# First stage of a hybrid attention block: two gates ahead of the memory, and keys written after the gates

## The chip, the cores and the metric

The kernel runs on one core of a Trainium2 chip. The time is that of one execution on the device, in microseconds (us). The core has a matrix engine (TensorE, PE in the profile; its weight loads are PEld), a vector engine (DVE), a scalar engine (ACT), GpSimd (POOL) and SyncE (SP), whose main work here is to issue DMAs. Each engine works through its own instructions in a fixed order and waits on semaphores that others raise. POOL issues some of the DMAs too, on a software queue.

## The reference

One layer for 1024 tokens of 1024 channels. After an RMS norm, one wide projection feeds three mixers and the merge gates; then comes an output projection with a residual, and a gated feed-forward part, which the change does not touch. All values are float32.

```python
h = _rmsnorm(x, norm_mix_g[l])
z = h @ w_in[l]
(hq, hf, hi, hg, fq, fk, fv, ff, mq, gate_logits) = jnp.split(z, pts, axis=-1)
...
mem_kv = _rmsnorm(mem, norm_mem_g[l]) @ mem_kv_w[l]      # 256 memory tokens, keys and values of 512
y_c = _memory_mixer(mq, mem_kv, mem_q_norm_g[l], mem_k_norm_g[l])
gates = jax.nn.sigmoid(gate_logits).reshape(B, T, 3, D_MODEL)
merged = gates[:, :, 0] * (y_a @ w_br_hgrn) + gates[:, :, 1] * (y_b @ w_br_fox) + gates[:, :, 2] * (y_c @ w_br_mem)
```

The 24 chunks of 128 gate channels (three branches of eight) and the queries of the memory mixer are plain projections of the normed x. The norm is applied late: a projection uses x times its gain, and the result is multiplied by the row rx of one scale for each token.

## The kernel before, in words

**Three matmuls for one.** To keep float32 accuracy, each operand is split into a high half (a cast, `cast`, L161, on ACT) and a low half (the difference, `split`, L169, on DVE). One product is then three matmuls in `mm3` (L155 to L157): high by high, high by low, low by high. A matmul here is 128x128 by 128x512. Where x is an operand, its halves are uh and ul (`x_chunk`, L316 on ACT and L317 on DVE), one pair of tiles for each of eight chunks of 128 channels.

**First stage.** The list SEQ sets the order of the steps in the program. In SEQ, k0 to k7 are the eight steps of the memory's projection (`kv_chunk`; four for the keys, four for the values, each with a weight tile wkv of 512 KB), x0 to x7 load and split a chunk of x, g0 and g1 split the weights of the first two gate chunks, s0 to s7 multiply one chunk of x with both (`gate_step`: 12 matmuls into four PSUM banks), mn, mk, mv and xn are the norm of the memory, its keys, its values and the norm of x (the squares of eight row tiles xr, L395, on ACT). All loads stand in one row on SP's queue. The split memory is umh and uml (L305, L306). `mem_keys` scales the keys (L365, L366, L367, L370), transposes them on TensorE (L375), scales them into mkf (L377), and POOL writes them to DRAM as kvd (L378). The values go the same way (L357, L358).

**What follows.** `spread_dma` (L323 to L327) makes the row rx: a transpose of the eight token columns, a copy on ACT, a write to DRAM and a load that repeats it over all partitions. `gate` multiplies a finished PSUM bank with rx (L420, DVE), takes a tanh (L421, ACT), and SP writes the tile gt, one of three, to DRAM (L431, L573). Two more gate chunks (the cover, `gates_early`) are computed while `differences` builds four families of differences of quarters of x, T1 to T4, from the raw tiles xk. Their halves are then operands of `dense_unit`, which computes two chunks of 128 channels at a time with seven products of quarters instead of eight (sums of weights s1 to s4, L474; PSUM snapshots fe, L466; products B11, B21, T1, T2, B22, T3, T4). The weights of a unit are loaded on POOL's queue (L499).

**What sets the order.** The program is recorded in the order of SEQ and of the code, and a scheduler then orders each engine's instructions by its own estimate; `tc.issue_after` keeps an instruction from being placed ahead of another. Tiles with the same tag share buffers, and a pool that is released makes its place free for the next one. The pool p0 of the first stage and the pool ps1 of the dense units lie on the same side: T1 to T4, s1, s2, fe and gt of ps1 come to lie where p0 had row tiles, split memory, mkf and others. Such a reuse is one more wait. In both kernels the place of s1 overlaps that of mkf.

## Time and profile before

| | |
|---|---|
| median of 3 runs | 1707.13 us (1705.72 to 1708.78) |
| profiled execution | 1707.23 us, its span 1705.5 us |
| granted TensorE clock | 1.0 |
| TensorE busy | 99% of the span, 8941 matmuls |
| DVE, ACT, POOL busy | 67%, 47%, 19% |
| DMA | 227.17 MB, mean 133 GB/s |

The span goes from the first to the last instruction. A row of the timeline is: start, duration, engine, line, operation, output and inputs, shapes, and in brackets the idle time just before it with what ended it. The durations of matmuls overlap, since they are pipelined: their pitch is the distance of two starts. On ACT and DVE the distance between starts is about 0.1 us less than a duration. A row by groups has a count, the busy time and the mean in ns. For DMAs, the time to landing is from the issue to the arrival of the last byte.

### The profile page before, as it was taken

Reading aid. Unit: us, or ns where it says so; the run is one execution under the profiler, and the core shown is the slowest. Engines: PE = TensorE matmul, PEld = TensorE weight load, DVE = VectorE, ACT = ScalarE, POOL = GpSimd, SP = SyncE. Lnnn points to the kernel's source line nnn. Section 1 sums busy time; section 2 is a strip of 40 time slices with the busy share of each in tenths; the row PEclk is TensorE's granted clock in tenths of the full one; section 3 lists DMA queues with packets and bytes.
Section 4 is the critical chain, followed back from the end, with each engine's and each line's share of the span. In section 5 each row is a group of like instructions: output and inputs, shape, how many; then the busy total and the mean of one; then the engine's idle time right before and its main releaser. Section 6 shows DMA issues by size and latency. Waiting matters only on the chain.

```text
span 1705.5 us, 24256 instructions
## 1 busy us (share of the span) xinstructions
PE 1689.9 (99%) x8941; PEld 1449.0 (85%) x8941; DVE 1142.3 (67%) x2044; ACT 808.9 (47%) x1436; POOL 325.7 (19%) x419
## 2 busy tenths in 40 slices
PE   8999999999999999999999999999999999999998
PEld 6888899989898998888888888788888888888887
DVE  7656545665666655786856845987787887775654
ACT  8634456655464553776531333644443444533432
POOL 0100022443433331553310000211111111100000
PEclk9999999999999999999999999999999999999999
DMA  9533232221212111100336552566445345494772
GB/s 361 182 132 112 76 133 85 77 92 45 95 53 87 52 57 56 67 28 17 102 128 210 166 185 99 161 174 173 144 146 142 118 141 155 167 357 150 244 273 87
DMA packets 83207, 227.17 MB, mean 133 GB/s; under 512 B 9728, under 2 KB 12424, under 8 KB 83088
## 3 DMA queue, kind: packets, MB, share of 16 engines
q1 hardware_dynamic: 65040, 161.12, 26.8%
q0 software_dynamic: 18048, 64.50, 13.1%
q8 instruction: 70, 1.15, 0.3%
q14 instruction: 49, 0.40, 0.1%
HBM read 180.72 MB, written 67.93 MB: 146 GB/s over the span
## 4 chain that ended last, share of the span: by engine, by line
PE 96%; DMA 2%; DVE 1%; ACT 1%; SPq 0%; issue 0%; POOL 0%; POOLq 0%; ACTq 0%
PE pp L155 21%; PE pp L157 21%; PE pp L156 21%; PE lg L157 4%; PE lg L155 4%; PE lg L156 4%; PE tr L156 2%; PE tr L157 2%; PE tr L155 2%; PE po L877 1%; PE lg L836 1%; PE lg L835 1%; PE po L876 1%; PE po L157 1%; PE po L155 1%; PE po L156 1%
## 5 line engine op out<-in xcount | busy, mean ns | idle before, releaser
L155 PE MATMUL pp<-uh,wh 128*128 128x512 f32 x412 | 163.2, 396 | 0.3 <-ACT wh L161 0.3
L156 PE MATMUL pp<-ul,wh 128*128 128x512 f32 x412 | 162.9, 395 | 0.0
L157 PE MATMUL pp<-uh,wl 128*128 128x512 f32 x412 | 162.4, 394 | 0.0
L156 PE MATMUL pp<-wl,uh 128*128 128x256 f32 (+1 forms) x512 | 146.2, 286 | 0.0
L157 PE MATMUL pp<-wh,ul 128*128 128x256 f32 (+1 forms) x512 | 145.9, 286 | 0.0
L155 PE MATMUL pp<-wh,uh 128*128 128x256 f32 (+1 forms) x512 | 145.5, 285 | 0.0
L161 ACT CAST wh<-s 128x512 fp32r<-128x512 f32 x113 | 68.4, 620 | 155.7 <-PE pp L156 77.6
L161 ACT CAST wh<-raw 128x1024 fp32r<-128x1024 f32 (+2 forms) x76 | 67.5, 890 | 101.3 <-PE pp L156 85.7
L161 ACT CAST wh<-rw 128x512 fp32r<-128x512 f32 x87 | 53.3, 620 | 97.6 <-PE pp L156 58.1
L155 PEld LDWEIGHTS pp<-wh,uh 128*128 128x128 f32 x512 | 97.3, 190 | 1.3
L156 PEld LDWEIGHTS pp<-wl,uh 128*128 128x128 f32 x512 | 97.4, 190 | 0.9
L157 PEld LDWEIGHTS pp<-wh,ul 128*128 128x128 f32 x512 | 97.4, 190 | 0.9
L1369 POOL DMA_DIRECT2D rw<-in_w_up x44 | 24.1, 555 | 384.9 <-ACT sqs L1304 163.0
L161 ACT CAST dwh<-wr 128x1024 fp32r<-128x1024 f32 (+1 forms) x41 | 40.2, 980 | 116.0 <-PE tr L156 39.2
L169 DVE TENSOR_TENSOR wl<-raw,wh 128x1024 fp32r<-128x1024 f32 (+2 forms) x75 | 78.0, 1041 | 22.0 <-ACT wh L161 21.7
L155 PEld LDWEIGHTS pp<-uh,wh 128*128 128x128 f32 x412 | 77.5, 188 | 15.3 <-ACT wh L161 0.7
L157 PEld LDWEIGHTS pp<-uh,wl 128*128 128x128 f32 x412 | 77.5, 188 | 15.1
L156 PEld LDWEIGHTS pp<-ul,wh 128*128 128x128 f32 x412 | 77.5, 188 | 14.5
L851 ACT ACTIVATE pt<-pt,st 128x128 f32<-128x128 f32 (+3 forms) x64 | 49.7, 777 | 39.8 <-DVE st L848 32.8
L169 DVE TENSOR_TENSOR dwl<-wr,dwh 128x1024 fp32r<-128x1024 f32 (+1 forms) x41 | 46.3, 1129 | 30.3 <-ACT dwh L161 30.2
L853 POOL TENSOR_SCALAR pt<-pt,st 128x128 f32<-128x128 f32 (+3 forms) x64 | 51.0, 797 | 78.0 <-DVE st L852 57.6
L161 ACT CAST ph<-tr 128x512 fp32r<-128x512 f32 (+1 forms) x80 | 41.8, 544 | 39.8 <-PE tr L865 14.5
(501 smaller groups left out, 5121.0 us busy)
## 6 DMA issues: line engine op xcount, KB each, us to landing
rw<-in_w_up POOLq DMA_DIRECT2D x44, 512.0 KB, 4.7
sd<-in_w_dn POOLq DMA_DIRECT2D x30, 512.0 KB, 6.0
br<-yd SPq DMA_DIRECT2D x30, 512.0 KB, 5.5
raw<-in_w_cm SPq DMA_DIRECT2D x26, 512.0 KB, 3.4
gd<-gt SPq DMA_DIRECT2D x48, 256.0 KB, 2.0
gt<-gd SPq DMA_DIRECT2D x48, 256.0 KB, 2.7
yd<-fc SPq DMA_DIRECT2D x44, 256.0 KB, 2.5
wr<-sd SPq DMA_DIRECT2D x20, 512.0 KB, 4.5
```

The lines of the kernel that those rows point to most:

```text
L155: PE.matmul(ps, lh, rh, start=first, stop=False, skip_group_check=more)
L156: PE.matmul(ps, lh, rl, start=False, stop=False, skip_group_check=more)
L157: PE.matmul(ps, ll, rh, start=False, stop=last, skip_group_check=more)
L161: return S.copy(out, in_)
L169: return (sub or V).tensor_sub(l, src, h.bitcast(F32))
L835: PE.matmul(ps[:, :w], qa[i][:, tsl], kh[i][:, s0:s0 + w], start=True, stop=False)
L836: fox_sets[p][3] = PE.matmul(ps[:, :w], qa[i][:, tsl], kl[i][:, s0:s0 + w], start=False, stop=True)
L851: S.activation(pt[:, :ns], pt[:, :ns], AF.Exp, bias=st[:, 2:3], accum_out=st[:, 3:4])
L853: G.tensor_scalar(pt[:, :ns], pt[:, :ns], st[:, 3:4], 0.0, ALU.mult, ALU.add)
L876: PE.matmul(o, vhl[:, sb, :], ph[:, src], start=(sb == 0), stop=False)
L877: PE.matmul(o, vhl[:, sb, :], pl[:, src], start=False, stop=last)
L1369: late["raw"] = G.dma_start(raw[:, 2 * i:2 * i + 2, :], src[:, 2 * i:2 * i + 2, :])
```

## The change

The first stage is put in another order and its loads with it.

- Nine matmuls of constants (`dull`) open TensorE's order.
- The two first gate chunks come before the memory. Their weights come as one new input, w_first, with the rows of both chunks for a channel side by side, in parts (`load_first`, `first_weights`); the first two chunks of x come and are split in halves. `gate_step` runs over the halves of the tokens first.
- The memory follows: all of it loaded with one DMA, split in eight steps (u0 to u7), then the eight steps k0 to k7. Row tiles of x have buffers of their own ("row"), four, as have the memory weights ("wkv").
- Four of the eight squares of the rows of x go to DVE (`tensor_tensor_reduce`).
- `mem_keys` is parted: `keys_out` (norm and scale) after the keys' four steps, and the transposes, the scaling into mkf and the write to DRAM at the end of SEQ, after the gates' evaluation.
- The first chunk of the cover is `first_cover`, in SEQ; the transpose for rx stands within it. `first_gates` follows it, all with gt tiles of p0.
- In `differences`, chunks 0 to 3 of x are no longer scaled by the gain. T1's halves take the gain while they are split, and T2 and T3 are formed with the negative gain column ngx.

The order of the built program: on ACT, the six tanh of the third, first and second gate chunks stand before the scaling of the second half of the keys into mkf. On POOL, the keys' write follows the first two weight loads of the dense units and the values' write. On DVE, the sum s1 follows; it waits for the keys' write, in whose place it lies. Behind s1 stand, in order: T1 low 0, s2, T1 low 1, a gate, T1 low 2, a difference for T2, T1 low 3, T3 low 0, a difference, T3 low 1 and 2, a difference, T3 low 3, a sum for T4, the low half of s1's weight.

```diff
...
+NDULL = 9
...
-SEQ = ("k0 k1 k2 k3 x0 x1 g0 x2 mr g1 k4 s0 s1 x3 s2 k5 x4 mn mk s3 k6 x5 s4 k7 mv x6 s5 x7 xn s6 s7").split()
+SEQ = ("w0 x0 s0 w1 x1 s1 w2 x2 s2 x3 s3 w4 x4 s4 x5 s5 x6 s6 x7 s7 u0 u1 u2 u3 mn u4 u5 u6 u7 k0 k1 k2 k3 me k4 k5 k6 k7 mv xn c0 ev mk").split()
+WFIRST = {0: (0, 1), 1: (1, 2), 2: (2, 4), 4: (4, 8)}
...
+    def row_tile(name, tag="wkv"):
+        return p0.tile([P, 2 * HB], F32, tag=tag, name=name, bufs=4)
+
+    for tag in ("row", "wkv"):
+        for i in range(4):
+            row_tile(f"{tag}{i}", tag)
+    umh = p0.tile([P, KC, NM], F32R, tag="umh", name="umh")
+    uml = p0.tile([P, KC, NM], F32R, tag="uml", name="uml")
+    mkf = p0.tile([P, 4, NM], F32, tag="mkf", name="mkf")
     mt = p0.tile([P, KC, NM], F32, tag="mt", name="mt")
-    def row_tile(name):
-        return p0.tile([P, 2 * HB], F32, tag="wkv", name=name, bufs=6)
-
-    wkv = [row_tile(f"wkv{q}") for q in range(4)]
-    mem_row = [row_tile(f"mr{i}") for i in range(2)]
-    wkv += [row_tile(f"wkv{q}") for q in range(4, 8)]
-    x_row = [row_tile(f"xr{i}") for i in range(6)]
-    x_row += [row_tile(f"xr{i}") for i in (6, 7)]
+
+    G.memset(mhalf, -0.5)
+    dull = p0.tile([P, P], F32, tag="line", name="dull")
+    G.memset(dull, 0.0)
+    for _ in range(NDULL):
+        PE.matmul(ps_tr()[:, :P], mhalf[:, 0:1].to_broadcast([P, P]), dull, start=True, stop=True)
+
+    wg = [row_tile(f"wg{i}") for i in range(2)]
+
+    def load_first(k):
+        k0, k1 = WFIRST[k]
+        sl = slice((k0 % 4) * 256, (k1 - 1) % 4 * 256 + 256)
+        SP.dma_start(wg[k // 4][:, sl], w_first[k // 4][:, sl])
+
+    def load_x(k, parts=1, between=None):
+        for i in range(parts):
+            sl = slice(i * T // parts, (i + 1) * T // parts)
+            SP.dma_start(xk[k][:, sl], xT[:, k, sl])
+            if between and i == 0:
+                between(k)
+
+    def load_wkv(q):
+        wkv.append(row_tile(f"wkv{q}"))
+        late["wkv"] = SP.dma_start(wkv[q], w_mkv[q])
+
+    def load_row(i):
+        nonlocal last_row
+        x_row.append(row_tile(f"xr{i}", "row"))
+        last_row = SP.dma_start(x_row[i], x_rows[i])
...
+    load_x(0, 2, load_first)
+    load_first(1)
+    load_x(1, 2)
+    load_first(2)
+    load_x(2)
+    load_first(4)
+    load_x(3)
+    load_x(4)
+    load_x(5)
+    load_x(6)
+    load_x(7)
+    SP.dma_start(mt, memT)
+    for i in range(2):
+        mem_row.append(row_tile(f"mr{i}"))
+        SP.dma_start(mem_row[i], mem_rows[i])
+    load_wkv(0)
+    load_wkv(1)
     SP.dma_start(ones, mats[:, P:P + 1])
-    rgw = []
-    for what in SEQ:
-        if what[0] == "x" and what != "xn":
-            k = int(what[1])
-            SP.dma_start(xk[k], xT[:, k, :])
-        elif what == "mr":
-            for i in range(2):
-                SP.dma_start(mem_row[i], mem_rows[i])
-        elif what[0] == "g":
-            br, j = order[int(what[1])]
-            rgw.append(raw_weights(w_cm[16 + 8 * br + j], KC * P))
-        elif what in ("k4", "k5", "k6", "k7"):
-            q = int(what[1])
-            SP.dma_start(wkv[q], w_mkv[q])
     SP.dma_start(ident, mats[:, 0:P])
-    for i in range(8):
-        last_row = SP.dma_start(x_row[i], x_rows[i])
-    G.memset(mhalf, -0.5)
+    for i in range(4):
+        load_row(i)
+    load_wkv(2)
+    load_wkv(3)
+    for i in range(4):
+        load_row(4 + i)
+        load_wkv(4 + i)
+    br, j = order[2]
+    cover_raw = raw_weights(w_cm[16 + 8 * br + j], KC * P)
...
+    def mem_chunk(k):
...
-        late["x_cast"] = S.activation(uh[k], xk[k], AF.Copy, scale=col(C_GX + k))
-        V.scalar_tensor_tensor(out=ul[k], in0=xk[k], scalar=col(C_GX + k), in1=uh[k].bitcast(F32),
-                               op0=ALU.mult, op1=ALU.subtract)
-
-    def spread_dma(r, rcol, row, name):
-
-        ps = ps_tr()
+        parts = 2 if k < 2 else 1
+        for i in range(parts):
+            sl = slice(i * T // parts, (i + 1) * T // parts)
+            S.activation(uh[k][:, sl], xk[k][:, sl], AF.Copy, scale=col(C_GX + k))
+            late["x_low"] = V.scalar_tensor_tensor(out=ul[k][:, sl], in0=xk[k][:, sl], scalar=col(C_GX + k), in1=uh[k][:, sl].bitcast(F32),
+                                   op0=ALU.mult, op1=ALU.subtract)
...
+    keys = []
+
+    def keys_out():
...
+        keys.append(mkt)
+
+    def mem_keys():
+        mkt = keys[0]
...
+    gps = [[ps_lg(), ps_lg()], [ps_tr(), ps_po()]]
+    gw = {}
+
+    def first_weights(k):
+        k0, k1 = WFIRST[k]
+        if k % 4 == 0:
+            gw[k // 4] = [wp.tile([P, 4 * 264], F32R, tag=t, name=t, bufs=3) for t in ("wh", "wl")]
+        sl = slice((k0 % 4) * 256, (k1 - 1) % 4 * 256 + 256)
+        split(S, gw[k // 4][0][:, sl], gw[k // 4][1][:, sl], wg[k // 4][:, sl])
 
     def gate_step(k):
-        for i in range(2):
-            for n in range(2):
+        h, l = gw[k // 4]
+        for n in range(2):
+            for i in range(2):
                 sl = slice(n * HB, (n + 1) * HB)
-                mm3(gps[i][n], gw[i][0][:, k, :], gw[i][1][:, k, :], uh[k][:, sl], ul[k][:, sl], k == 0, k == KC - 1)
+                ws = slice((k % 4) * 256 + i * P, (k % 4) * 256 + (i + 1) * P)
+                mm3(gps[i][n], h[:, ws], l[:, ws], uh[k][:, sl], ul[k][:, sl], k == 0, k == KC - 1)
...
+            if i % 2:
+                V.tensor_tensor_reduce(out=x_row[i], in0=x_row[i], in1=x_row[i], op0=ALU.mult, op1=ALU.add, scale=1.0,
+                                       scalar=0.0, accum_out=rt[:, i:i + 1])
+            else:
+                late["square"] = S.activation(x_row[i], x_row[i], AF.Square, accum_out=rt[:, i:i + 1])
...
+    cover = gates_early(NCOVER - 1)
+
+    def first_cover():
+        wh, wl = weights(None, (KC, P), cover_raw)
+        late["keys"] = late["split cast"]
+        spread = ps_proj()
+        pss = [ps_proj(), ps_proj()]
+        for n, ps in enumerate(pss):
+            sl = slice(n * HB, (n + 1) * HB)
+            for k in range(KC):
+                late["cover"] = mm3(ps, wh[:, k, :], wl[:, k, :], uh[k][:, sl], ul[k][:, sl], k == 0, k == KC - 1)
+                if (n, k) == (0, 2):
+                    with tc.issue_after(late["cover"].ins):
+                        spread_dma(rx, rt, p0.tile([P, P], F32, tag="line", name="line")[:8, :], "rx", spread)
+        for n, ps in enumerate(pss):
+            SP.dma_start(gd[2, n], gate(n, ps))
+
+    def first_gates():
+        for n in range(2):
+            for i in range(2):
+                SP.dma_start(gd[i, n], gate(n, gps[i][n]))
+
+    steps = dict(k=kv_chunk, x=x_chunk, w=first_weights, s=gate_step, u=mem_chunk)
+    named = dict(mn=mem_norm, me=keys_out, mk=mem_keys, mv=mem_values, xn=x_norm, ev=first_gates, c0=first_cover)
...
-        b = []
-        for k in range(4):
-            for t in (k, k + 4):
-                with tc.issue_after(late["square" if t > 3 else "x_cast"].ins):
-                    S.activation(xk[t], xk[t], AF.Copy, scale=col(C_GX + t))
-            b.append([xk[k + 4 * c][:, n * HB:(n + 1) * HB] for c in range(2) for n in range(2)])
+        b = [[xk[k + 4 * c][:, n * HB:(n + 1) * HB] for c in range(2) for n in range(2)] for k in range(4)]
+        for t in range(4, 8):
+            with tc.issue_after(late["keys"].ins):
+                S.activation(xk[t], xk[t], AF.Copy, scale=col(C_GX + t))
         for k, (b11, b12, b21, b22) in enumerate(b):
-            V.tensor_sub(b11, b11, b12)
-            family_block("T1", k, b11)
+            with tc.issue_after(late["x_low"].ins):
+                V.tensor_sub(b11, b11, b12)
+            h, l = (t[:, k, :] for t in fam["T1"])
+            S.activation(h, b11, AF.Copy, scale=col(C_GX + k))
+            V.scalar_tensor_tensor(out=l, in0=b11, scalar=col(C_GX + k), in1=h.bitcast(F32), op0=ALU.mult, op1=ALU.subtract)
         yield
-        with tc.issue_after(first_gates.ins):
+        with tc.issue_after(first_gate.ins):
             for k, (t1, b12, b21, b22) in enumerate(b):
-                V.scalar_tensor_tensor(out=t1, in0=t1, scalar=-1.0, in1=b22, op0=ALU.mult, op1=ALU.subtract)
+                V.scalar_tensor_tensor(out=t1, in0=t1, scalar=ngx[:, k:k + 1], in1=b22, op0=ALU.mult, op1=ALU.subtract)
                 family_block("T2", k, t1)
         yield
-        with tc.issue_after(first_gates.ins):
+        with tc.issue_after(first_gate.ins):
             for k, (t2, b12, b21, b22) in enumerate(b):
-                V.tensor_sub(b12, b22, b12)
+                V.scalar_tensor_tensor(out=b12, in0=b12, scalar=ngx[:, k:k + 1], in1=b22, op0=ALU.mult, op1=ALU.add)
                 family_block("T3", k, b12)
...
```

More of the change, by code (lines that the diff above doesn't have):

```diff
@@ L413, in tile_block @@
     mqd = tc.dram_tile([4, P, T], F32, name="mqd")
+    home = {"pool": p0}
     def gate_tile():
@@ L607, in tile_block @@
     wsplit[:] = [S, V]
-    cover, families = gates_early(NCOVER), differences()
-    next(cover)
+    families = differences()
+    with tc.issue_after(late["wkv"].ins):
+        next(cover)
     next(families)
```

65 lines of the change are left out of this document (22 added, 43 removed).

## The prediction

> **What bounds the kernel now.** I read the page's shares and slices first, then the chain that ended last, then the waits of TensorE, and then the first 100 us of the timeline, engine by engine.
>
> ```profile
> span 1705.5 us, 24256 instructions
> PE 1689.9 (99%) x8941; PEld 1449.0 (85%) x8941; DVE 1142.3 (67%) x2044; ACT 808.9 (47%) x1436; POOL 325.7 (19%) x419
> PE   8999999999999999999999999999999999999998
> PE 96%; DMA 2%; DVE 1%; ACT 1%; SPq 0%; issue 0%; POOL 0%; POOLq 0%; ACTq 0%
> ```
>
> TensorE is busy from end to end and is 96% of the chain, so the time is the number of its matmuls times their pitch, plus its waits. The built order of the changed kernel has the same matmuls plus nine blank ones, and from the first product with the fourth family of differences (T4, the end of the first dense unit) its TensorE order is that of before, instruction by instruction. So the change is worth what it does to the time at which that product starts. Before, from the timeline:
>
> ```profile
> 5.29 1.22 PE L155 MATMUL tr<-wh,umh 128*128 128x512 f32 x2 [5.29 <-ACT wh L161]
> 7.16 0.63 PE L156 MATMUL tr<-wl,umh 128*128 128x512 f32 x1
> 7.58 0.63 PE L157 MATMUL tr<-wh,uml 128*128 128x512 f32 x1
> 9.63 0.39 PE L156 MATMUL tr<-wl,umh 128*128 128x512 f32 x1
> 11.81 0.50 PE L156 MATMUL tr<-wl,umh 128*128 128x512 f32 x1 [0.53 <-DVE wl L169]
> 25.16 0.50 PE L157 MATMUL po<-uh,gl 128*128 128x512 f32 x1 [0.52 <-DVE gl L169]
> 85.21 0.50 PE L155 MATMUL pp<-T2h,wh 128*128 128x512 f32 x1 [0.68 <-ACT fe L466]
> 88.97 0.50 PE L155 MATMUL pp<-uh,wh 128*128 128x512 f32 x1 [0.28 <-ACT wh L161]
> 99.54 0.39 PE L155 MATMUL pp<-T4h,wh 128*128 128x512 f32 x1
> 99.77 0.39 PE L156 MATMUL pp<-T4l,wh 128*128 128x512 f32 x1
> ```
>
> The pitch is 0.227 us (99.54 to 99.77, and the same over the whole stretch), but 0.42 until about 9.4 us. Ahead of T4 stand 384 matmuls of 512 columns and 9 transposes of about 0.1: 87.1 + 1.0 = 88.1 us. The kernel before starts at 5.29 and reaches T4 at 99.54, so 94.25 - 88.1 = 6.2 us are lost behind the start: 2.1 to the slow pitch (some ten matmuls by 0.2), and the rest to waits, 1.4 near 11 us, 0.9 near 25 and 1.5 between 84 and 89. No opening, however good, can gain more than about 6 us here.
>
> **The change, part by part.** *Opening: two gates by channels of x, before the memory.* Loads come in the order of issue, so I match bytes. The halves and parts of x and of the gate weights that now come first sum to the same bytes as pieces of before: 0.46 MB up to the first gate weights, 1.11 MB up to the first half of chunk 1 of x, 1.64 MB up to chunk 2's weights (before: the first memory weights, the third piece of the memory, the second memory weights).
>
> ```profile
> 4.62 0.62 ACT L161 CAST wh<-wkv 128x512 fp32r<-128x512 f32 x1 [0.26 <-DMA wkv<-in_w_mkv]
> 8.21 0.91 ACT L305 ACTIVATE umh<-mt,cv 128x256 fp32r<-128x256 f32 x2 [1.60 <-DMA mt<-in_memT]
> 9.45 1.05 ACT L161 CAST wh<-wkv 128x1024 fp32r<-128x1024 f32 x1 [0.33 <-DMA wkv<-in_w_mkv]
> 12.10 1.05 ACT L161 CAST wh<-wkv 128x1024 fp32r<-128x1024 f32 x1 [0.35 <-DMA wkv<-in_w_mkv]
> 20.00:30.00 10.00, 9.48 (x41) 7.25 (x40) 6.78 (x10) 9.69 (x15) 0.90 (x2) 1.00 1.03 420
> L316 ACT ACTIVATE uh<-xk,cv 128x1024 fp32r<-128x1024 f32 x8 | 9.0, 1150 | 0.5 <-DMA xk<-in_xT 0.4
> L317 DVE SCALAR_TENSOR_TENSOR ul<-xk,cv,uh 128x1024 fp32r<-128x1024 f32 x8 | 10.0, 1280 | 0.2
> L298 DVE TENSOR_SCALAR hgc<-cv 128x1 f32<-128x1 f32 x1 | 0.2, 154 | 2.5 <-DMA cv<-in_vec 2.5
> L305 ACT ACTIVATE umh<-mt,cv 128x256 fp32r<-128x256 f32 x8 | 3.7, 502 | 3.4 <-DMA mt<-in_memT 3.4
> ```
>
> Each of these rows idled until its DMA landed, so the gate weights land at 4.6, chunk 1 of x at 8.2 and chunk 2 (2.16 MB, between the 1.64 of 9.45 and the 2.42 of 12.10) at 11.2. A cast of 256 columns is 0.5: the first gate matmul starts at about 5.1 to 5.2, as before. Step 0 is 12 matmuls, 2.7 us; step 1 then waits until 8.8; step 2 waits for 11.2 + 1.1 = 12.3, and 0.4 more for the low half behind it. From then on x comes at 0.42 MB per us (the 420 of that row), 1.25 us a chunk against 2.7 of matmuls: steps 2 to 7 run without waits to 29.1. Lost: 29.1 - 5.1 - 21.8 = 2.2 us, 1.3 less than the slow pitch and the waits near 11 us cost before. The nine blank matmuls are to bring the full pitch earlier. They cost nothing and bring little: at half pitch step 0 ends at 10.2 instead of 8, while step 2 waits until 12.3 anyway. Their price has no row; eight stand ahead of the first real one, between 0.1 each (the pitch of transposes) and 0.63 each, thus done between 2 and 6.3 us, and a first step that starts 1.1 late is covered by the same wait. The finer pieces of x, the constant column and the constant scale on DVE (0.15 us each near 2.6 us) lie in that wait too.
>
> *The memory behind the gates.* Bytes ahead of memory weights 1, 2, 4 and 5 are now 10.1, 11.7, 13.2 and 14.8 MB; at 0.418 from 12.10 on they land at 30.4, 34.2, 38.0 and 41.7.
>
> ```profile
> L161 ACT CAST wh<-wkv 128x1024 fp32r<-128x1024 f32 x7 | 7.3, 1047 | 0.8 <-DMA wkv<-in_w_mkv 0.7
> L169 DVE TENSOR_TENSOR wl<-wkv,wh 128x1024 fp32r<-128x1024 f32 x7 | 8.6, 1223 | 2.5 <-ACT wh L161 2.5
> L395 ACT ACTIVATE xr<-xr 128x1024 f32<-128x1024 f32 x8 | 8.4, 1053 | 0.2 <-DMA xr<-in_x_rows 0.2
> L367 DVE TENSOR_REDUCE mkr<-mkt 128x4 f32<-128x512 f32 x2 | 1.3, 679 | 0.0
> ```
>
> Cast plus low half are 2.3 us behind the landing. Step 1 waits 0.4 for its low half, step 2 0.2 and 0.7, step 5 0.5 for a cast that ACT does behind the key scales, their squares and a square of x (0.5 + 1.1 + 0.5 + 0.5 us), and then 1.7 for its low half, which stands on DVE behind a reduction and one of the four row squares that move from ACT to DVE. With five restarts of 0.1 the memory takes 21.8 + 4.0, to 54.9. A row square on DVE has no row: between 1.2 (ACT's price with its read of the sum) and 2.6 (a product and two reductions); I take 1.3, as its form is that of the 1.28 us row above, and 2.6 would add 1.1 us to step 5.
>
> *The cover, the row of scales and the gate writes.* The third gate runs from 54.9 to 65.8 without a wait. What follows rests on these rows:
>
> ```profile
> 69.70 2.49 DVE L590 SCALAR_TENSOR_TENSOR xk<-xk,xk 128x512 f32<-128x512 f32 x4
> 72.10 2.50 DVE L595 TENSOR_TENSOR xk<-xk,xk 128x512 f32<-128x512 f32 x4
> L582 ACT ACTIVATE xk<-xk,cv 128x1024 f32<-128x1024 f32 x8 | 8.5, 1140 | 0.0
> L421 ACT ACTIVATE gt<-gt 128x512 f32<-128x512 f32 x8 | 4.8, 628 | 7.2 <-DVE gt L420 7.2
> gd<-gt SPq DMA_DIRECT2D x7, 256.0 KB, 2.0
> 43.76 0.55 POOL L378 DMA_DIRECT2D kvd<-mkf  x1
> kvd<-mkf POOLq DMA_DIRECT2D x1, 512.0 KB, 8.5
> kvd<-mvf POOLq DMA_DIRECT2D x1, 512.0 KB, 4.8
> DVE gt L420 <- DMA gd<-gt: 1.5, 1, 1.5
> L377 ACT ACTIVATE mkf<-tr,mgk 128x512 f32<-128x512 f32 x2 | 1.2, 670 | 0.0
> 59.65 0.35 SPq L326 DMA_DIRECT2D rx_d<-row  x1
> 60.94 0.35 SPq L327 DMA_DIRECT2D rx<-rx_d  x1
> 64.55 1.29 DVE L420 TENSOR_TENSOR gt<-lg,rx 128x512 f32<-128x512 f32 x2 [4.07 <-DMA rx<-rx_d]
> ```
>
> The scale row rx needs its transpose after 9 matmuls of the cover, its copy at 57.4, and then 1.3 us (59.65 to 60.94) and 3.6 (to 64.55) of DMA: 62.3, before the cover's end. Its move on SP's queue thus costs nothing. Of the eight scalings of x on ACT (1.14 each) four fall away, as the scale now goes into T1's halves and into two of the differences; these keep the two-operand form of the 0.6 us rows on DVE. ACT waits for others here, so it gains nothing.
>
> The keys decide. Before, they left for DRAM at 43.76. Now the second half of them is scaled on ACT behind the six gates of x, and those share three tiles, each free only 2.0 us after its write was issued (the 1.5 us wait of that row is one such). Second half of the cover done 66.1; its gate on DVE 66.7; half of the keys and the tanh on ACT 67.8; write 69.7; the fifth and sixth gate on DVE 70.9; tanh 71.5; rest of the keys 72.2; then the write, for which I take 4.8: 77.2 with the queue's issue. Who waits for it: the sum s1 of the first dense unit lies where the keys lay, so DVE's next instruction in the built order stands until 77.2, and behind it, in order, stand the low halves of T1, T2 and T3, half the differences and the low half of s1's own weight, which is the 15th after it. DVE takes 0.605 each (four in 2.4): 77.2 + 15 x 0.605 + 0.7 = 87.0. TensorE comes to that point after the cover, eight transposes, the fourth gate and two products: 65.8 + 0.5 + 10.9 + 0.4 + 5.4 + 0.5 = 83.5. It waits 3.5. (The next unit's weight loads stand behind the keys' write on POOL's queue; before they were read near 88, now some 8 us later, so 73 is early enough for their issue.) Then it is DVE that it follows: the sum s3, 28th behind s1, is done at 77.2 + 16.9 + 0.7 = 94.8 and cast at 95.5, which starts the T3 product; 48 matmuls stand from there to T4 (10.9), with a wait of 0.7 for the next cast and 0.3 of restarts: T4 at 107.4.
>
> *Sum.* 107.4 - 99.5 = 7.9 us later, and nothing behind T4 moves against TensorE. The profiled execution took 1707.23 (1.7 outside its span), the median of the three is 1707.13: 1715.0.
>
> The Trainium skill, "DMA: Bandwidth & Descriptors", section "Anatomy of one DMA — SWDGE (gpsimd) path", fits such a write as 2.0 us plus its bytes at 436 GB/s; as an estimate that is 3.2 us for the keys, against 4.8 and 8.5 in the rows, and the sum would be 1713.4. The rows here are higher in both cases, so they decide.
>
> **Rivals.** (1) The wait on the keys is hidden, so no slower: it takes a start of s1 at 73.6 or earlier, 1.4 us after the write is issued, or a different place of s1. Then TensorE keeps its pitch after 54.9 and T4 comes at 5.1 + 88.1 + 2.2 + 4.0 + about 0.5 = 99.9: 1707.5, within 0.2%. For it: before, that wait did not show. Against: both rows of that write are over three times too long. (2) The write takes 8.5 as its other row, 3.7 more: 1718.7. For it: that is the same tile; against: loads of x filled the DMA then, and here only gate writes run. (3) The early x comes at the 0.42 of later instead of the rate of the first 9 us: 1.4 less, 1713.6. Against: all early rows show the slow rate whatever the pieces. Faster than before it can only be if rival 1 holds and the opening's 2.2 or the memory's 4.0 are not there either: T4 near 95.5, 1703; that is the remainder.
>
> **How the numbers follow.** The forecast has 0.61, rival 2 0.12, rival 3 0.12, rival 1 0.10, the remainder 0.05. Some 3.4 us, 0.2%, is what a measurement here tells from no change. Faster 0.05, same 0.10, slower 0.85. The range goes below rival 3 by the errors of a ledger with some 20 rounded steps, which may add up, and above rival 2 by part of the 1.1 us of row squares: 1709 to 1719.5.
>
> **What would show it.** TensorE's first gate matmul near 5.2, waits on casts of x until about 12.5, then none to 29; waits on the low halves of memory weights near 32, 36 and 46; DVE idle some 3 us before s1 with the keys' write as its releaser; TensorE idle 3 to 4 us at the first T1 product, released by a low half, and T4 near 107. The prediction is wrong if the keys' write lands within 2 us, if DVE's pitch behind s1 is not 0.6, or if T4 stands before 103.

## The result: 7.3 us slower

The changed kernel takes 1714.15 us (median of 6 runs, 1712.1 to 1715.8), the kernel before 1706.88 in the same comparison (1705.7 to 1709.5): ratio of the means 1.0039, 95% interval 1.0026 to 1.0052. The prediction was 1715.0, range 1709.0 to 1719.5. The sum came out; one of its main causes did not.

The page of the changed kernel, its span, shares and chain:

```profile
span 1712.3 us, 24286 instructions
PE 1695.5 (99%) x8959; PEld 1452.1 (85%) x8959; DVE 1148.9 (67%) x2056; ACT 802.4 (47%) x1427; POOL 326.6 (19%) x420
PE 93%; DMA 3%; DVE 2%; ACT 1%; issue 0%; SPq 0%; POOL 0%; DVEq 0%; ACTq 0%; POOLq 0%
```

TensorE is as busy as before, and the chain has 3 points less of it: waits. The timeline of TensorE shows where they lie (a row: start, duration, ..., and in brackets the idle time just before it with what ended it):

```profile
5.44 0.50 PE L157 MATMUL lg<-uh,wh 128*128 128x512 f32 x1 [0.88 <-ACT wh L163]
...
29.00 0.62 PE L157 MATMUL pp<-wh,umh 128*128 128x512 f32 x2
33.12 0.50 PE L158 MATMUL pp<-wl,umh 128*128 128x512 f32 x1 [0.52 <-DVE wl L171]
36.86 0.50 PE L158 MATMUL pp<-wl,umh 128*128 128x512 f32 x1 [0.53 <-DVE wl L171]
45.37 0.50 PE L157 MATMUL pp<-wh,umh 128*128 128x512 f32 x1 [0.51 <-ACT wh L163]
47.43 0.50 PE L158 MATMUL pp<-wl,umh 128*128 128x512 f32 x1 [1.33 <-DVE wl L171]
...
83.60 0.39 PE L157 MATMUL lg<-T1h,wh 128*128 128x512 f32 x1
87.20 0.51 PE L159 MATMUL lg<-T1h,wl 128*128 128x512 f32 x1 [2.76 <-DVE wl L171]
95.93 0.50 PE L157 MATMUL pp<-T3h,wh 128*128 128x512 f32 x1 [1.92 <-ACT wh L163]
98.15 0.63 PE L159 MATMUL pp<-T3h,wl 128*128 128x512 f32 x1
98.58 0.63 PE L157 MATMUL pp<-T3h,wh 128*128 128x512 f32 x1
108.90 0.39 PE L157 MATMUL pp<-T4h,wh 128*128 128x512 f32 x1
```

The gates of x end at 29.0 and cost 1.8 us beyond their 96 matmuls at 0.227. The 96 memory matmuls lose 4.5 (the 193rd starts at 55.27: 26.27 - 21.76), the cover and the products behind it 1.1, of which their nine transposes are 1.0. The last 72 matmuls ahead of T4 take 83.60 to 108.90, 25.3 us instead of 16.3: 9.0 lost, against 1.6 before. T4 starts 9.4 us later than before (108.90 against 99.54), while the span is 6.8 longer.

What the other engines do there, from their timelines:

```profile
58.38 0.62 ACT L163 CAST wh<-raw 128x512 fp32r<-128x512 f32 x1 [1.03 <-DMA raw<-in_w_pair]
58.91 0.25 ACT L362 COPY line<-pp 8x128 f32<-8x128 f32 x1
59.18 0.35 SPq L364 DMA_DIRECT2D rx_d<-line  x1
62.13 0.35 SPq L365 DMA_DIRECT2D rx<-rx_d  x1
66.59 1.29 DVE L463 TENSOR_TENSOR gt<-pp,rx 128x512 f32<-128x512 f32 x2 [1.68 <-DMA rx<-rx_d]
73.08 0.67 ACT L420 ACTIVATE mkf<-tr,mgk 128x512 f32<-128x512 f32 x1
73.65 2.55 ACT L652 ACTIVATE T1h<-xk,cv 128x512 fp32r<-128x512 f32 x4
74.05 0.54 POOL L421 DMA_DIRECT2D kvd<-mkf  x1 [15.30 <-ACT mkf L420]
77.00 0.69 DVE L545 TENSOR_TENSOR s<-raw 128x512 f32<-128x512 f32 x1 [1.24 <-DMA kvd<-mkf]
86.46 0.69 DVE L171 TENSOR_TENSOR wl<-s,wh 128x512 fp32r<-128x512 f32 x1
94.54 0.69 DVE L545 TENSOR_TENSOR s<-raw 128x512 f32<-128x512 f32 x1
```

The first row with s is s1, the last s3. DVE idles only 1.24 us for the keys' write, which takes 2.9 by the list of DMA issues (the last number, from issue to landing):

```profile
kvd<-mkf POOLq DMA_DIRECT2D x1, 512.0 KB, 2.9
```

The same instructions of the kernel before stand elsewhere:

```profile
53.61 0.69 DVE L474 TENSOR_TENSOR s<-raw 128x512 f32<-128x512 f32 x1 [1.34 <-DMA raw<-in_w_pair]
57.17 2.18 ACT L161 CAST T1h<-xk 128x512 fp32r<-128x512 f32 x4
57.99 2.49 DVE L169 TENSOR_TENSOR T1l<-xk,T1h 128x512 fp32r<-128x512 f32 x4
```

Before, s1, s2 and T1's low halves were done ahead of the row rx, in time in which DVE has nothing else; now they come some 20 us later, in a stretch in which DVE has little time left: from 66.6 to 95 it is idle for 3.4 us only. From the first gate to s3 it starts 39 instructions, before 32; six of the seven more are s1, s2 and T1's low halves. s3 itself stands at 94.54 instead of 85.33, 9.2 us later, as T4 does.

One more term shows in the windows of the changed kernel (busy time of each engine in a stretch; the seventh field is the granted clock):

```profile
89.50:92.90 3.40, 2.79 (x11) 1.53 (x9) 3.40 (x7) 2.49 (x5) 0.88 (x2) 1.00 0.54 170
92.90:96.30 3.40, 1.26 (x5) 0.60 (x4) 3.30 (x6) 1.58 (x3) 1.07 (x2) 1.00 1.01 345
96.30:99.70 3.40, 3.13 (x8) 2.09 (x7) 3.40 (x7) 2.28 (x4) 0.00 (x0) 0.50 0.82 331
```

For 3.4 us, right behind a stretch in which TensorE worked 1.26 of 3.40, it had half its clock: the pitch of 0.43 in the rows near 98. What that costs, the runs below bracket: the 48 matmuls from the first T3 product to T4 take 11.6 and 11.9 us in the two kernels whose half clock is over by then (scale_undone, keys_early), 12.8 to 13.5 in those with one such stretch among them (13.0 here), so 1 to 2 us. The kernel before has no such stretch between 9.5 us and its end.

### The profile page after: what moved, and what is told of

It is laid out like the page before. It is cut to its first block, busy times and chain, and to the rows that moved or that the text cites. A ratio compares the mean times of both kernels' runs of the same rounds, so it can differ in the third digit from the quotient of the medians.

```text
span 1712.3 us, 24286 instructions
## 1 busy us (share of the span) xinstructions
PE 1695.5 (99%) x8959; PEld 1452.1 (85%) x8959; DVE 1148.9 (67%) x2056; ACT 802.4 (47%) x1427; POOL 326.6 (19%) x420
## 4 chain that ended last, share of the span: by engine, by line
PE 93%; DMA 3%; DVE 2%; ACT 1%; issue 0%; SPq 0%; POOL 0%; DVEq 0%; ACTq 0%; POOLq 0%
PE pp L159 20%; PE pp L157 20%; PE pp L158 20%; PE lg L157 4%; PE lg L158 4%; PE lg L159 4%; PE tr L159 2%; PE tr L158 2%; PE tr L157 2%; PE po L945 1%; PE lg L904 1%; PE lg L903 1%; PE po L944 1%; PE tr L932 1%; PE lg L1134 1%; PE po L157 1%
## 5 line engine op out<-in xcount | busy, mean ns | idle before, releaser
L163 ACT CAST wh<-s 128x512 fp32r<-128x512 f32 x113 | 68.4, 619 | 150.4 <-PE pp L158 72.2
L163 ACT CAST wh<-raw 128x1024 fp32r<-128x1024 f32 (+2 forms) x76 | 67.7, 890 | 109.4 <-PE pp L158 82.1
L909 DVE CUSTOM_DVE_ANT_0 pt<-lg,nf 128x512 f32<-128x512 f32 (+2 forms) x80 | 41.6, 527 | 28.4 <-PE lg L904 14.1
```

The costliest lines, as they stand in the source:

```text
L163: return S.copy(out, in_)
L909: V.tensor_tensor_reduce(out=pt[:, s0 + lo:s0 + hi], in0=ps[:, lo:hi], in1=bias, op0=ALU.add, op1=ALU.max, scale=1.0, scalar=-3e38, accum_ ...
```

## The experiments

All twelve in one table. "T4" is the start of the first T4 product in the profiled run, "lost" what the last 72 matmuls ahead of it take beyond 16.3 us, "half clock" the time at half clock between 12 us and T4, from the clock records of the trace. The profile is one execution, the median is over 4 to 11 (28 of the kernel before in the last group).

| kernel | T4 | lost | half clock | median | ratio to before (95%) |
|---|---|---|---|---|---|
| before | 99.5 | 1.6 | 0 | 1706.3 to 1707.1 | |
| changed | 108.9 | 9.0 | 3.4 | 1714.15 | 1.0039 (1.0026 to 1.0052) |
| keys_place | 109.5 | 8.3 | 6.8 | 1713.97 | 1.0041 (1.0026 to 1.0055) |
| scale_undone | 109.8 | 9.6 | 6.8 | 1715.15 | 1.0050 (1.0035 to 1.0065) |
| fill_wait | 109.2 | 9.7 | 6.8 | 1714.00 | 1.0043 (1.0028 to 1.0058) |
| memory_first | 104.3 | 9.0 | 3.4 | 1709.51 | 1.0016 (1.0007 to 1.0026) |
| gates_pool | 108.9 | 9.7 | 6.8 | 1715.53 | 1.0053 (1.0038 to 1.0068) |
| keys_early | 108.9 | 8.5 | 3.4 | 1715.79 | 1.0052 (1.0037 to 1.0067) |
| keys_early_gates_pool | 105.8 | 4.8 | 3.4 | 1712.58 | 1.0035 (1.0025 to 1.0046) |
| no_blanks | 109.4 | 9.1 | 6.8 | 1716.10 | 1.0054 (1.0039 to 1.0069) |
| order_only | 107.3 | 5.0 | 6.8 | 1711.53 | 1.0023 (1.0014 to 1.0032) |
| order_and_memory | 100.9 | 4.2 | 3.4 | 1706.63 | 0.9995 (0.9986 to 1.0004) |
| all_and_pool | 104.6 | 7.5 | 6.8 | 1709.71 | 1.0016 (1.0007 to 1.0024) |
| before_pool | 104.4 | 6.5 | 3.4 | 1712.55 | 1.0032 (1.0019 to 1.0044) |

**Is it the wait on the keys' write?** (keys_place)

```diff
-    for tag in ("row", "wkv"):
-        for i in range(4):
-            row_tile(f"{tag}{i}", tag)
+    for i in range(4):
+        row_tile(f"row{i}", "row")
+    mkf = p0.tile([P, 4, NM], F32, tag="mkf", name="mkf")
+    for i in range(4):
+        row_tile(f"wkv{i}", "wkv")
...
-    mkf = p0.tile([P, 4, NM], F32, tag="mkf", name="mkf")
```

> The changed kernel with the tile mkf of the keys allocated between the row tiles and the memory weights, so that the sum s1 lies where the split memory was and waits for no write; the order of every engine's work stays. Theory A (the prediction): the keys' write holds DVE and through it TensorE, so without it the waits of the first dense unit go, T4 starts near 100 to 101 instead of 108.9, and the time falls to about 1707 (7 us less). Theory B (from the trace of the changed kernel, where DVE idles only 1.24 us before s1): DVE's 28 us of work behind the first gate at 66.6 decide, and the write costs 0.3 to 1.3 us: s1 near 75.8, T4 between 107.5 and 108.6, the time 1713 to 1714; 1711.5 to 1712.5 if the stretch of half clock near 97 goes with it.

```profile
67.48 1.29 DVE L464 TENSOR_TENSOR gt<-pp,rx 128x512 f32<-128x512 f32 x2
76.56 0.68 DVE L546 TENSOR_TENSOR s<-raw 128x512 f32<-128x512 f32 x1
86.52 0.69 DVE L171 TENSOR_TENSOR wl<-s,wh 128x512 fp32r<-128x512 f32 x1
```

The wait is gone (no bracket at s1), and the time is the same. This execution had half clock in the memory's steps too and its first gate 0.9 us later (67.48 instead of 66.59), and s1's low half still comes at the time of the changed kernel: the write was worth 0.8 us, not 7. Theory A, the prediction's, is out.

**Did taking four scalings off ACT gain nothing?** (scale_undone)

```diff
-        for t in range(4, 8):
+        for t in range(8):
             with tc.issue_after(late["keys"].ins):
                 S.activation(xk[t], xk[t], AF.Copy, scale=col(C_GX + t))
...
-            S.activation(h, b11, AF.Copy, scale=col(C_GX + k))
-            V.scalar_tensor_tensor(out=l, in0=b11, scalar=col(C_GX + k), in1=h.bitcast(F32), op0=ALU.mult, op1=ALU.subtract)
+            family_block("T1", k, b11)
...
-                V.scalar_tensor_tensor(out=t1, in0=t1, scalar=ngx[:, k:k + 1], in1=b22, op0=ALU.mult, op1=ALU.subtract)
+                V.scalar_tensor_tensor(out=t1, in0=t1, scalar=-1.0, in1=b22, op0=ALU.mult, op1=ALU.subtract)
...
-                V.scalar_tensor_tensor(out=b12, in0=b12, scalar=ngx[:, k:k + 1], in1=b22, op0=ALU.mult, op1=ALU.add)
+                V.tensor_sub(b12, b22, b12)
```

> The changed kernel with all eight chunks of x scaled on ACT as before, T1 split from the scaled difference, and T2 and T3 formed with -1 again. The prediction's step (ACT waits for others there, so taking four scalings away gains nothing): T4 within 0.5 us of 108.9 and the time within 1 us of 1714.2. Rival: the four scalings of 1.07 us stand on ACT ahead of the copy of the scale row (58.9 in the changed kernel), so rx lands about 4 us later than 66.5, the gates and all of DVE's work behind them follow, and T4 comes at 111 to 113, the time at 1716 to 1718.

The gates do move as the rival said: the first one starts at 70.23 instead of 66.59. s3 stands 2.0 us later (96.57), but T4 moves by 0.9 only: the half clock lies ahead of the T3 product here (88.2 to 95.0), and the 48 matmuls from there to T4 take 11.6 us instead of 13.0. The median moves by 1.0, inside the intervals. So the scalings are worth about 1 us here, and perhaps 2 where the half clock lies as in the changed kernel.

**Does the idle time near 84 bring the half clock?** (fill_wait)

```diff
+    blanks = {"T1": 14}
...
+            late["product"] = PE.matmul(ps, wh[:, ks], bh, start=first, stop=False, skip_group_check=more)
+            with tc.issue_after(late["product"].ins):
+                bank = ps_tr()
+                for _ in range(n):
+                    last = PE.matmul(bank[:, :P], mhalf[:, 0:1].to_broadcast([P, P]), ident, start=True, stop=True)
+            with tc.issue_after(last.ins):
+                PE.matmul(ps, wh[:, ks], bl, start=False, stop=False, skip_group_check=more)
+                late["product"] = PE.matmul(ps, wl[:, ks], bh, start=False, stop=False, skip_group_check=more)
```

> The changed kernel with 14 blank matmuls of 128 columns (two passes each, about 3 us) on TensorE behind the first matmul of the T1 product, where it waits 2.8 us for the low half of s1's weight. If the half clock between 96 and 99.5 us comes from the idle time just before it, the granted clock stays 1.0 there and T4 starts near 107.5 instead of 108.9, the time some 1 us lower. If it comes from the later waits (1.9 us near 94 to 96) or has nothing to do with idle time, the half clock is still there and T4 is at 108.9 or up to 1 us later.

```profile
84.00:87.40 3.40, 3.40 (x29) 3.27 (x28) 3.40 (x6) 1.00 (x2) 0.00 (x0) 1.00 0.00 1
90.80:94.30 3.50, 2.00 (x7) 0.78 (x5) 3.40 (x6) 2.10 (x4) 1.06 (x2) 1.00 0.99 363
94.30:97.70 3.40, 2.60 (x5) 1.66 (x6) 3.40 (x7) 2.28 (x4) 0.00 (x0) 0.53 1.01 347
```

The wait near 84 is filled and the half clock is there all the same, for 6.8 us. So it is not that wait; it follows the thin stretch ahead of the T3 product, as in the changed kernel. T4 and the median stay within 0.3 us of the changed kernel's.

**The memory's waits** (memory_first)

```diff
-... k0 k1 k2 k3 me k4 k5 k6 k7 ...
+... k0 k1 k2 k3 k4 k5 me k6 k7 ...
...
-        mem_row.append(row_tile(f"mr{i}"))
+        mem_row.append(row_tile(f"mr{i}", "row"))
...
-    load_wkv(0)
-    load_wkv(1)
+    for q in range(4):
+        load_wkv(q)
...
     for i in range(4):
         load_row(i)
-    load_wkv(2)
-    load_wkv(3)
+        load_wkv(4 + i)
     for i in range(4):
         load_row(4 + i)
-        load_wkv(4 + i)
...
+            with tc.issue_after(late["split cast"].ins):
+                S.activation(mkt[:, m, :], pkv[0][m], AF.Copy, scale=rm[:, m:m + 1])
```

> The changed kernel with four memory weights loaded ahead of the rows of x (the two rows of memory lie in the row tiles), and the norm of the keys placed behind the splits of the sixth memory weight. The waits of 4.5 us in the memory's steps (near 33, 37, 45 and 47) should go; the cover starts near 51 instead of 55, the row rx and the gates come 2 to 3 us earlier and T4 at 105 to 106.5. If DVE's order behind the gates only depends on the gates and the keys, the whole gain arrives: 1711 to 1712. If the keys' write sets the dense unit, it arrives too, since the keys move with it; if the waits return as others in the cover, the time stays at 1714.

TensorE's timeline has no wait between 28 and 54 us, the 193rd matmul starts at 50.7 instead of 55.3, T4 at 104.3, and the time is 1709.5. The whole 4.6 us arrive at the end. The dense unit loses 9.0 as before: the two losses add up. The gain is larger than expected (1711 to 1712). The built order also moved the keys: their second half is scaled ahead of the six tanh, the write is issued at 63.80, and s1 (72.59) waits for nothing. T1's first half still stands right behind the last tanh, and the 9.0 are lost all the same.

**What holds T1 back?** (gates_pool, keys_early, and both) On ACT, T1's first half stands right behind the last instruction that touches p0 (73.08 and 73.65 above). Two kinds of tiles make p0 live that long: the gate tiles and the keys. So each was taken out alone, and both.

```diff
 gates_pool:
+    pg = Rounded(tc, name="pg", bufs=1, side="right", reuse_waits="tile")
     p0 = Rounded(tc, name="p0", bufs=1, side="right", reuse_waits="tile")
...
-    home = {"pool": p0}
+    home = {"pool": pg}
...
-    home["pool"] = ps1
 keys_early (in first_cover; keys_half(hh, bank) is one turn of the loop of mem_keys, the second writes kvd):
         spread = ps_proj()
+        keys_half(0, spread)
...
+                if (n, k) == (0, 1):
+                    with tc.issue_after(late["cover"].ins):
+                        keys_half(1, spread)
-                if (n, k) == (0, 2):
+                if (n, k) == (0, 3):
```

> The changed kernel with the gate tiles gt in a pool of their own that outlives the pool p0; the keys stay behind the gates. Theory B2: the built order puts nothing of the dense units' pool ps1 ahead of the last use of p0, and by that T1's halves, s1 and s2 come behind the gates and the keys; the keys' scaling at 73 is still p0's last use here, so nothing is gained: T1's first half near 73.7, T4 within 1 us of 108.9, time 1713 to 1715. Rival: the gate tiles alone hold T1 back: T1's halves before 66 and T4 near 103.

> The changed kernel with the keys transposed, scaled and written within the first matmuls of the cover, some 15 us earlier; the gate tiles stay in p0. Theory A (the prediction): the write has long landed when s1 comes, its wait is gone and T4 falls to 100 to 104, the time to 1706 to 1709. Theory B2: the gates' last tanh near 73 is then the last use of p0, T1's halves stay behind it, and T4 stays within 1 us of 108.9 to 110, the time 1714 to 1715.

> Both: the keys within the cover's first matmuls, and the gate tiles in a pool of their own. Theory B2: p0's last use is then the copy of the scale row near 59 to 62, T1's halves, s1 and s2 go ahead of the gates, and T4 comes at 102 to 105.5 (the upper end with a stretch of half clock), the time at 1707.5 to 1711. Theory A: no different from keys_early.

The rows on ACT ahead of T1, first with the gates' own pool, then with early keys, then with both:

```profile
72.40 0.67 ACT L421 ACTIVATE mkf<-tr,mgk 128x512 f32<-128x512 f32 x1
75.11 0.63 ACT L465 ACTIVATE gt<-gt 128x512 f32<-128x512 f32 x1 [2.04 <-DVE gt L464]
75.65 2.55 ACT L652 ACTIVATE T1h<-xk,cv 128x512 fp32r<-128x512 f32 x4
```

```profile
73.71 1.95 ACT L463 ACTIVATE gt<-gt 128x512 f32<-128x512 f32 x3 [1.63 <-DVE gt L462]
75.56 2.55 ACT L656 ACTIVATE T1h<-xk,cv 128x512 fp32r<-128x512 f32 x4
```

```profile
64.92 0.25 ACT L363 COPY line<-pp 8x128 f32<-8x128 f32 x1
65.08 2.56 ACT L656 ACTIVATE T1h<-xk,cv 128x512 fp32r<-128x512 f32 x4
```

One alone gains nothing (1715.5 and 1715.8, just above what was expected): with the gates' own pool T1 comes behind the keys' scaling (and one more tanh, for which ACT waits), with early keys behind the last tanh. Both bring T1 ten us forward, right behind the copy of the scale row, which is then p0's last use. The first low half of s1's weight comes at 72.4 instead of 86.5, the wait of 2.76 at the T1 product is gone, and T4 comes 3.1 us earlier. Of these, 1.5 us are given back between 220 and 230 us, where the built order is another one with the extra pool (one wait of 1.9 at 228 us, for a copy on ACT); so the time missed the expected 1707.5 to 1711. keys_early is also a second answer to theory A: its write was issued 15 us earlier, and T4 is at 108.9. It is not a clean one, as the copy of the scale row there stands behind a cast that waits for a weight until 63.88, and the first gate comes at 69.53, 2.9 us later; with both edits it comes at 69.98, in order_only below at 71.46. That these two gain in spite of it makes the case for T1's place the stronger.

**Without the blank matmuls** (no_blanks)

```diff
-NDULL = 9
+NDULL = 0
```

> The changed kernel without its nine blank matmuls. The prediction's step (they bring little, as step 2 waits for its part of x until 12.3 anyway): the pitch is 0.43 until 9 to 10 us, the gates of x end within 0.7 us of 29.0, T4 within 1 us of 108.9 and the time within 1 us of 1714.2. Rival: the full pitch from the start is worth the 2 us that the slow pitch cost the kernel before, so 1716.

The pitch is 0.43 until 9.2 us (0.23 from 5.9 in the changed kernel), and the gates of x end at 29.3 instead of 29.0. That is all that the opening shows. The median is 1.95 higher, though, near the rival's 1716, but with intervals that overlap; in the profiled run, 2.6 us longer, 0.5 of it is there at T4 and the rest comes by a longer wait and a half clock stretch near 241 us, which the changed kernel's run does not have. keys_place, with its nine blanks, has the same stretch, so it does not need their absence. Why all four runs lie above 1715 stays open.

**The order alone, and with the memory** (order_only, order_and_memory) As keys_early, with the third gate chunk's evaluation and first_gates recorded behind the release of p0, as in the kernel before; then with the edit of memory_first, and the transpose for rx in a bank of its own.

```diff
-... mv xn c0 ev mk
+... mv xn c0
...
-        for n, ps in enumerate(pss):
-            SP.dma_start(gd[2, n], gate(n, ps))
+        cover_banks.extend(pss)
...
     families = differences()
+    for n, ps in enumerate(cover_banks):
+        SP.dma_start(gd[2, n], gate(n, ps))
+    first_gates()
+    first_gate = late["gate"]
+    next(families)
     with tc.issue_after(late["wkv"].ins):
         next(cover)
-    next(families)
```

> The changed kernel with the keys within the cover's first matmuls, and the six gates recorded behind the release of p0, with the gate tiles of ps1, as in the kernel before; no extra pool, so that nothing behind the first dense unit is ordered anew. Theory B2: T1's halves go at 60 to 65, T4 at 102 to 106 (as with keys early and a pool for the gates, 105.8), and the 1.5 us which that kernel gave back near 230 us are not lost here: 1710 to 1711.5. Theory A: no different from keys_early, 1714 to 1716.

> The last edit together with the memory's loads and norm of memory_first, and the transpose for rx two matmuls earlier in a bank of its own. If the change's loss is the sum of the memory's waits (4.6 us) and of the late T1, s1 and s2 (3 us), and nothing else, then the loss is gone: T4 at 99.5 to 102, the time within 1.5 us of the kernel before, 1705.5 to 1708. If the two overlap (an earlier memory only lets TensorE wait for DVE), T4 stays at 103 to 104 and the time at 1709.

order_only loses 5.0 instead of 9.0 in the last 72 matmuls and is 2.6 us faster than the changed kernel, though its profiled run had an extra half clock stretch in the memory (47.9 to 51.3). Its T4 and time lie just above the expected range. With the memory's loads in order as well, T4 comes at 100.9 and the time is that of the kernel before: in the main, the loss is these two things. That the row rx comes earlier there too (first gate at 65.49 instead of 71.46) has a part in it that no run separates. What the dense unit still loses (4.2) is at the T3 product, where TensorE waits 1.88 us for the cast of s3, and part of it at half clock; an earlier s3 on DVE was not tried.

**Work to POOL** (all_and_pool, before_pool)

```diff
-                family_block("T3", k, b12)
+                family_block("T3", k, b12, G if k in (0, 1, 2, 3) else None)
...
-            family_block("T4", k, t4[k])
+            family_block("T4", k, t4[k], G if k in (2, 3) else None)
...
 all_and_pool only:
-            G.dma_start(t, src[:, 2 * i:2 * i + 2, :])
+            (SP if first else G).dma_start(t, src[:, 2 * i:2 * i + 2, :])
```

> The same, with four low halves of T3 and two of T4 on POOL instead of DVE (1.3 us each by the row of such a split in the kernel before), and the first two weights of the dense unit loaded on SP's queue, so that they do not stand behind the writes of keys and values. If DVE's work behind the first gate decides the waits at the T3 product, these go, T4 comes at 96.5 to 99.5, and the time is 1703 to 1706, below the kernel before. If POOL and DVE hinder each other, or the POOL splits come late, T4 stays near 101.

> The kernel before with the same six low halves on POOL, nothing else. It waits 1.5 us near 84 to 91 for DVE's work (T4 at 99.5). If that is all there is to gain, T4 comes at 98 to 99.3 and the time is within 1.5 us of the kernel before, so that what all_and_pool gains comes from the opening and the memory; rival: as much is gained here as there, 1703 to 1705.

POOL and then DVE in before_pool:

```profile
73.44 7.33 POOL L169 TENSOR_TENSOR T3l<-xk,T3h 128x512 fp32r<-128x512 f32 x4 [19.25 <-ACT T3h L161]
```

```profile
74.44 0.68 DVE L420 TENSOR_TENSOR gt<-pp,rx 128x512 f32<-128x512 f32 x1
75.04 1.18 DVE L599 SCALAR_TENSOR_TENSOR t4s<-xk,xk 128x512 f32<-128x512 f32 x1
77.85 1.77 DVE L169 TENSOR_TENSOR T2l<-xk,T2h 128x512 fp32r<-128x512 f32 x1
79.55 1.78 DVE L599 SCALAR_TENSOR_TENSOR t4ta<-xk,xk 128x512 f32<-128x512 f32 x1
```

The four splits take 7.3 us on POOL instead of the 5.2 of four at 1.3, and DVE's own instructions with both operands in SBUF take 1.2 to 1.8 instead of 0.68 while they run. s3 comes 2.0 us later (87.34), and TensorE then waits 4.8 us at the T2 product. That wait has a second cause, on ACT in before_pool:

```profile
88.10 0.62 ACT L161 CAST wh<-s 128x512 fp32r<-128x512 f32 x1 [2.51 <-DVE s L474]
88.63 0.58 ACT L466 COPY fe<-pp 128x512 f32<-128x512 f32 x1
```

The two copies for which the T2 product waits (88.63 and 89.11) stand behind the cast of s3 here; in the kernel before they stand ahead of it, at 84.58 and 85.06. So the built order turned DVE's 2 us into most of the 4.8. The edit made the kernel before 5.5 us slower; all_and_pool, where the first two weights also moved to SP's queue, is 3.1 slower than order_and_memory. Both expectations missed, and how much is due to POOL and DVE hindering each other and how much to the order was not separated. No version here beats the kernel before.

## Why the prediction was right, and where it was wrong

*Reading the change at T4.* It held in kind: 9.4 us at T4, 7.6 at the last matmul, 6.8 in the span. That nothing behind T4 moves against TensorE failed by 2.6 us: 1.8 at three places where TensorE waited for others before and now waits less (near 230, 1085 and 1089 us of before), 0.8 behind the last matmul. The last of the three places, of before, then of after:

```profile
1089.12 0.50 PE L157 MATMUL pp<-B11h,wl 128*128 128x512 f32 x1 [1.41 <-DVE fa L1461]
```

```profile
1096.73 0.50 PE L159 MATMUL pp<-B11h,wl 128*128 128x512 f32 x1 [0.80 <-DVE fa L1529]
```

*Opening.* Predicted first gate matmul 5.1 to 5.2 and end at 29.1; measured 5.44 and 29.00. Right. The blanks bring the full pitch from the first matmuls on and 0.3 us, as "cost nothing and bring little" said for this stage.

*Memory.* Predicted waits near 32, 36 and 46 with 4.0 lost; measured 4.5, at the four places above (2.9 of it idle, the rest in slower matmuls around the waits). Right, and in memory_first, without them, the time is 4.6 us lower. The row square on DVE, which had no row, took 1.22 and a read of 0.08: the 1.3 that was taken.

*The row rx.* Predicted at 62.3, measured at 66.5, so this step was wrong by 4 us: the copy on ACT stood behind a cast that waited for a weight (58.38), the write took 2.95 instead of 1.3 and the load 4.4. The forecast had the first gate done before the cover's end. Instead the gates begin at 66.59, the fourth waits until 70.03 for the tile of the first, and the sixth ends at 72.5 instead of 70.9. So the miss reached the keys with some 1.5 us; what it cost at T4 no run shows alone. The step "ACT waits for others here, so it gains nothing" belongs here too: with all eight scalings on ACT the first gate came 3.6 us later (scale_undone).

*The keys' write.* Two sizes missed in opposite directions: the second scaling ends at 73.75 instead of 72.2, and the write takes 2.9 us instead of 4.8. The estimate from the Trainium skill, "DMA: Bandwidth & Descriptors", section "Anatomy of one DMA — SWDGE (gpsimd) path", was 3.2 and the nearer one. Issued before the gates, the same write took 3.2 (all_and_pool) to 7.9 (before_pool), and 8.5 in the kernel before. That s1 started at 77.00 for 77.2 predicted is luck: a scaling forecast 1.5 too early and a write forecast 1.9 too long cancel.

*"The keys decide".* This is the step that failed. It took DVE to stand idle for 3 us before s1; it was idle for 1.24, because four differences and a gate filled the time, and keys_place shows that without the wait T4 does not come earlier. What decides is DVE's order: s1, s2 and T1's low halves, which it had done before while it waited for rx, were built behind p0's last use, at 73. Of the 9.2 us by which s3 is later, 2.0 are the later first gate, 5.2 more work between it and s3, and 1.9 more idle time, of which the keys' write is 1.24. The T3 product follows the start of s3 by 1.4 us in the changed kernel and in nine of the others, so TensorE follows DVE there, as the forecast said. The steps behind s1 were counted by 0.605 from an end that happened to be right, so the low half at 87.15 (for 87.0), the T3 product at 95.93 (for 95.5) and a wait of 2.76 (for 3.5) came out.

*DVE's pitch.* The forms with a column of constants as scalar were taken to keep the 0.69 of the plain ones. They take 0.75 (L657, L653 and L662: 747, 745 and 750 ns; 686 before with a number as scalar). Twelve of them make 0.7 us (part of the 5.2).

*T4.* 108.9 for 107.4. 0.4 of the 1.5 us is the later start of the T3 product; 1.1 lie between it and T4, where the half clock lies, which was in no part of the sum.

*The rivals.* Rival 1 fell with its reason: hiding the write does not help. Rival 2 fell (2.9, not 8.5). Rival 3 fell: the casts of x stand where the slow early rate puts them, chunk 2's at 10.9.

So the opening, the memory and the order behind s1 were forecast rightly, and the keys' write was a wrong cause in the right place. The sum was 7.9; it missed 1.5 at T4 and had 2.6 too much behind it. That 1715.0 lies within 0.9 of the median is in part luck, as these cancel.

## What to carry to other kernels

A late step costs more than its own time when its tiles share a pool: in these kernels the built order put nothing of the next pool ahead of the old pool's last use, so two late users moved ten other instructions (T1's eight halves, s1 and s2) out of idle time, and removing one of the two gained nothing. Before blaming a wait that ends last, add up what the waiting engine has to do around it: a wait of 1.2 us within 28 us of work is not the bound. And check where the idle time of that engine lies; here DVE had 9 us free between 55 and 66, which is where the work belonged.

## What was not expected of the hardware

**Half clock after thin stretches.** In 13 of the 14 kernels profiled here, TensorE fell to half its clock ahead of T4, always for 3.41 or 6.83 us. The windows above show what lies ahead of it: a stretch in which TensorE is idle for much of the time. No idle time there was longer than 3 us in the changed kernel. The same waits in the memory brought it in one execution and not in another; keys_place, then the changed kernel:

```profile
43.60:47.00 3.40, 1.60 (x6) 0.67 (x4) 2.98 (x5) 3.40 (x5) 0.00 (x0) 1.00 0.34 137
47.00:50.40 3.40, 3.36 (x8) 2.69 (x9) 3.00 (x5) 0.33 (x1) 2.60 (x2) 0.51 0.01 2
```

```profile
45.10:48.50 3.40, 1.80 (x7) 1.20 (x8) 3.40 (x6) 2.62 (x4) 0.30 (x1) 1.00 0.06 22
48.50:51.90 3.40, 3.40 (x17) 2.81 (x16) 2.67 (x4) 1.87 (x2) 3.40 (x2) 1.00 0.00 0
```

The Trainium skill, "TensorE: Matmul & The Clock Gate", section "Part 1: The HAM clock gate (the "warmup" mystery)", has a free-running window of 3413 ns and a fall to half clock after an idle one. The lengths agree with the window; that a stretch used by about half can be enough is what these runs add.

The falls of one run lie whole multiples of 3.413 us apart (keys_place: 47.08, 98.28 and 241.64), so the stretches can be cut exactly. In the 3.41 us right ahead of the 17 falls before T4, TensorE was busy for 0.00 to 1.82 us (1.27 in the changed kernel, 1.70 in fill_wait, 1.57 in the memory of keys_place). In the other such stretches at full clock between 12 us and T4 it was busy for 1.78 or more (1.83 in the memory of the changed kernel). So the same waits brought the fall or not by how they lay on that grid. Two falls behind T4 do not fit: near 241 us, in keys_place and no_blanks, they came after 2.57 and 2.35 us. The matmuls there have 256 columns or one, so busy time may not be what counts; that was not tried. Waits of 0.5 to 1.3 us that lie close together can thus cost 1 to 2 us more, in some executions.

**POOL against DVE.** DVE's 0.68 us became 1.2 to 1.8 while POOL worked on operands in SBUF, and stayed 0.68 for the gate, which reads PSUM (before_pool, 74.44 and 76.15). The Trainium skill, "SBUF — State Buffer", section "SBUF: two separate sides", tells of one port pair that DVE and POOL lock against each other, for DVE instructions with two inputs in SBUF. The rows agree. For the gate this rests on these two rows.
